# One-level Strassen in the up-projection of a transformer trunk, and the feed-forward in two phases

## The chip, the cores and the metric

The kernel runs on one NeuronCore of a Trainium2 chip, in one launch. The metric is the device time of one execution in microseconds. Engines are named as the profile names them: PE (TensorE, matmuls; PEld its weight loads), DVE (VectorE), ACT (ScalarE), POOL (GpSimd), SP (SyncE, which here only issues DMAs).

## What is computed

An inference step of a two-layer encoder for 1024 prompt rows and 8 x 16 sample rows (1152 rows of 1024 in all). Each layer has attention (layer 0: a sliding window with sinks; layer 1: a band over keys and values that all rows share) and a convolutional feed-forward. Every sub-layer gets a shift and a scale from a conditioning vector ("ada") and is closed by a LayerNorm. All is float32. The feed-forward, which the change is about (`w_up` goes from 1024 to 2 x 2816 channels, the convolution is causal over rows, by channel and three wide, `w_down` goes from 2816 back to 1024):

```python
def conv_ffn(h, prev, w_up, conv_w, conv_b, w_down):
    u = h @ w_up
    ...
    for tap in range(CONV_W):
        y = y + conv_w[tap] * ue[:, tap:tap + T]
    a, g = jnp.split(y, 2, axis=-1)
    out = (jax.nn.gelu(g) * a) @ w_down
    return out, ue[:, T:]
...
h = x * (1 + sc_f) + sh_f
f, conv_rows = conv_ffn(h, None if prompt else state_conv[l], w_up[l], conv_w[l], conv_b[l], w_down[l])
x = layer_norm(DEEPNORM_ALPHA * x + (1 + g_f) * f, ln_g[l, 1], ln_b[l, 1])
```

## The kernel before

Rows are 9 tiles of 128 (tiles 0 to 7 the prompt, tile 8 the samples). A product of float32 operands is three products of split operands: `split` makes a high part (a cast to fp32r, on ACT) and a low part (source minus high part, on DVE or POOL), and a product takes low x high, high x low and high x high.

The kernel is a straight program. A scheduler sets the order of the instructions on each engine ahead of the run, from its own estimates; each engine then runs its list strictly in order. All DMAs stand in SP's list. Stages: start and attention 0, output projection 0 (`out_proj`, which ends in a LayerNorm, `norm_tail`, and writes `H`, the split and transposed input of the feed-forward), feed-forward 0 (`ffn`), attention 1, output projection 1, feed-forward 1.

`H` is [part, channel block, 1152 rows]. `wload` brings 512 KB of weights into one of two staging slots (`ws`), casts them on ACT and subtracts on POOL (L151, L162) into one of four pairs of slots (`wh`, `wl`). In `ffn`, `up(j, gg)` multiplies one 128-channel tile of `w_up` (half gg of the GEGLU) with all rows in three blocks of 384 (`mmT`, L274, 24 matmuls a block), straight into convolution (`conv`: one activation on ACT, two taps on DVE that read PSUM), GELU and product (L1035, L1037); the result stays in SBUF. `down(g)` multiplies two finished tiles j with their rows of `w_down` (`dmm`, L1062, 6 matmuls of 512 columns for each tile of rows and half) and adds them to `acc` in SBUF (L1053 on DVE), for all nine tiles of rows; it runs among the next tiles' up-projection. `down_last` takes the last two j with the gate folded into the weights and finishes tile after tile with the LayerNorm. `pregate` adds the residual (L1121, L1122). `ada` makes the conditioning: seven of them, each 16 loads of 512 KB and 32 matmuls (L216). One stands at the start, two run beside attention 0, four (3 to 6) beside feed-forward 0 in steps (`step`, every `wload` takes 0.72 of a step).

Of the kernel before, what the change touches and what calls it, by code (L numbers as in the profile page):

```python
# [10 lines left out]
F32 = mybir.dt.float32  # L11
# [4 lines left out]
D = 1024  # L16
# [15 lines left out]
LO = ((0, 1, 2, 8, 3, 4, 5, 6, 7), (0, 1, 2, 3, 4, 5, 8, 6, 7))  # L32
UP = ({0: (0, 1), 2: (2,)}, {0: (0, 1), 3: (2,)})
LV = (0, 1, 2, 8, 3, 4, 5, 6, 7)
BGA = 0.33
BGF = 0.72
# [52 lines left out]
class Trunk:  # L89
    def __init__(self, ctx, tc, I, O):  # L90
# [10 lines left out]
        self.H = mem.tile([128, 2, 8, TOK], F32R, name="H")  # L101
# [21 lines left out]
        self.sm = ca.ring(16, 2)  # L123
        self.PS = psp.tile([128, 8, 512], F32, name="PS")
# [5 lines left out]
        self.oN = dr.tile([7, 128, 1024], F32, name="oN")  # L130
        self.oSD = dr.tile([8, 128, 128], F32, name="oSD")
# [136 lines left out]

    def mmT(self, w, out, s0, n):
        H = self.H  # L270
        i = 0
        for a, p in ((1, 0), (0, 1), (0, 0)):
            for k in range(8):
                self.nc.tensor.matmul(  # L274
                    out[:, 0:n], w[a][:, k * 128 : k * 128 + 128], H[:, p, k, s0 : s0 + n], start=i == 0, stop=i == 23
                )
                i += 1

    def mmX(self, out, t0, ws, kn, n):
# [3 lines left out]
        for j, w in enumerate(ws):  # L283
            for p, a in ((1, 0), (0, 1), (0, 0)):
                for k in range(kn):
                    self.nc.tensor.matmul(  # L286
                        out[:, 0:n],
                        H[:, p, j * kn + k, t0 : t0 + 128],
# [57 lines left out]
    def attention(self, l, wk):  # L346
# [5 lines left out]
        self.X1 = self.x1p.tile([128, 9216], F32R, name=f"x1att{l}", tag="x1")  # L352
        xa = Arena(self.X1)
# [50 lines left out]
        ka = Arena(self.F, (11136, 0)[l])  # L404
# [43 lines left out]
        def qblock(c, bi, w):  # L448
# [13 lines left out]
            for a in range(2):  # L462
# [23 lines left out]
        def scores(x):  # L486
# [9 lines left out]
            for qi in (2 * g, 2 * g + 1):  # L496
# [3 lines left out]
                q = qs(c, a, slice(0, 128), qi * 128, 128)  # L500
# [88 lines left out]
        def normalise(c, a, h):  # L589
# [146 lines left out]
        for i, x in enumerate(work):  # L736
# [12 lines left out]
            self.step(BGA)  # L749
# [601 lines left out]
```

## Time and profile before

| | us |
|---|---|
| median of 3 runs (2999.06 to 3001.47) | 3001.14 |
| span of the profiled execution | 3005.7 |
| PE busy | 2859.9 (95%) |
| DVE, ACT, POOL busy | 1563.2, 1162.4, 904.0 |
| mean granted clock of TensorE | 0.974 |

The profiled execution's span is 4.6 us longer than the median of the runs. In rows of groups the last three parts are busy us and mean ns of one, idle time before them, and what ended that. In rows of stages the numbers are busy us of PE, PEld, DVE, ACT and POOL with instruction counts, then the granted clock, the DMA engines' mean busy share and GB/s. A mean duration of a matmul is longer than what it costs, since matmuls are pipelined; costs are taken from stretches of many.

### The profile page before, as it was taken

What the parts mean: (1) busy time and instruction counts of PE and PEld (TensorE: products, weight loads), DVE (VectorE), ACT (ScalarE), POOL (GpSimd) and SP (SyncE); (2) the same over time, 40 slices, a digit from 0 to 9 for tenths busy, and PEclk for the clock granted to TensorE, in tenths of its full rate; (3) what the DMA queues carried; (4) which work ended last, traced back from release to release, by engine and by line L of the source; (5) the groups of instructions that cost most, each with busy time, mean ns of one, the idle gap of its engine ahead of it and who ended that gap; (6) DMA issues with size and microseconds to landing.
All of it is one profiled execution on the core that took longest, in us unless ns stands there. A gap on an engine that the chain in (4) does not pass through costs nothing.

```text
span 3005.7 us, 43456 instructions
## 1 busy us (share of the span) xinstructions
PE 2859.9 (95%) x16582; PEld 2548.1 (85%) x16582; DVE 1563.2 (52%) x3416; ACT 1162.4 (39%) x2608; POOL 904.0 (30%) x661
## 2 busy tenths in 40 slices
PE   7998889999999999998999999989999999999996
PEld 4986668888888898997999888867899999999985
DVE  4365658424444444458312677666624444444467
ACT  3464643332222222224435666652442222222224
POOL 2121322322222322253561111321422222222252
PEclk8998989999999999999999999999999999999998
DMA  8645353622222222222785467763311111111121
GB/s 299 186 145 155 107 158 111 224 88 78 99 88 81 101 76 74 79 84 101 266 296 180 116 158 196 189 203 108 131 43 41 43 44 45 43 43 43 42 78 66
DMA packets 175536, 353.96 MB, mean 118 GB/s; under 512 B 34632, under 2 KB 91784, under 8 KB 174944
## 3 DMA queue, kind: packets, MB, share of 16 engines
q1 hardware_dynamic: 175328, 351.19, 36.4%
q8 instruction: 130, 2.13, 0.3%
q14 instruction: 78, 0.64, 0.1%
HBM read 285.22 MB, written 75.35 MB: 120 GB/s over the span
## 4 chain that ended last, share of the span: by engine, by line
PE 70%; DVE 7%; ACT 3%; DMA 2%; issue 2%; POOL 2%; SPq 0%; DVEq 0%; ACTq 0%; POOLq 0%
PE PS L274 40%; PE PS L1062 16%; PE PS L286 7%; PE PS L559 1%; PE PS L540 1%; PE PS L216 1%; DVE acc L1122 1%; PE PS L514 1%; DVE F L480 1%; ACT F L784 1%; DMA oSD<-C 1%; DVE F L946 1%; PE PS L517 1%; PE PS L874 0%; POOL acc L1121 0%
## 5 line engine op out<-in xcount | busy, mean ns | idle before, releaser
L274 PE MATMUL PS<-H,wh 128*128 128x384 f32 x5472 | 1051.8, 337 | 0.3 <-DVE H L162 0.3
L274 PEld LDWEIGHTS PS<-H,wh 128*128 128x128 f32 x5472 | 964.2, 189 | 21.3 <-issue 5.4
L162 POOL TENSOR_TENSOR wl<-ws,wh 128x1024 fp32r<-128x1024 f32 x167 | 405.8, 2435 | 643.3 <-ACT wh L151 601.4
L274 PE MATMUL PS<-H,wl 128*128 128x384 f32 x2736 | 561.8, 342 | 38.0 <-POOL wl L162 9.8
L986 DVE SCALAR_TENSOR_TENSOR F<-PS,F 128x256 f32<-128x256 f32 (+2 forms) x704 | 352.7, 511 | 463.5 <-ACT F L983 453.1
L274 PEld LDWEIGHTS PS<-H,wl 128*128 128x128 f32 x2736 | 485.9, 190 | 71.7 <-issue 15.7
L1062 PE MATMUL PS<-wh,X 128*128 128x512 f32 x1320 | 420.1, 395 | 8.5 <-DVE acc L1053 3.2
L1053 DVE TENSOR_TENSOR acc<-acc,PS 128x512 f32<-128x512 f32 x324 | 221.6, 686 | 295.7 <-PE PS L1062 292.7
L1037 POOL TENSOR_TENSOR F<-F 128x384 f32<-128x384 f32 x132 | 136.4, 1033 | 729.5 <-ACT F L1035 719.9
L1062 PEld LDWEIGHTS PS<-wh,X 128*128 128x128 f32 x1320 | 245.1, 188 | 60.1 <-issue 9.2
L983 ACT ACTIVATE F<-PS,F 128x384 f32<-128x384 f32 x264 | 177.9, 674 | 243.7 <-PE PS L274 240.0
L151 ACT CAST wh<-ws 128x1024 fp32r<-128x1024 f32 x174 | 180.7, 1049 | 143.4 <-PE PS L1062 47.0
L1062 PE MATMUL PS<-wl,X 128*128 128x512 f32 x660 | 217.1, 394 | 0.0
L162 DVE TENSOR_TENSOR X<-F,X 128x384 fp32r<-128x384 f32 x110 | 125.4, 1140 | 117.1 <-ACT X L151 116.9
L1020 ACT COPY PS<-PS 128x2 f32<-128x2 f32 x176 | 25.6, 145 | 407.2 <-PE PS L274 388.2
L286 PE MATMUL PS<-wh,H 128*128 128x256 f32 (+1 forms) x936 | 173.1, 315 | 7.7 <-DVE H L162 7.2
L286 PEld LDWEIGHTS PS<-wh,H 128*128 128x128 f32 x936 | 137.3, 194 | 18.8 <-DVE H L162 7.8
L1062 PEld LDWEIGHTS PS<-wl,X 128*128 128x128 f32 x660 | 124.6, 189 | 28.5
L596 POOL TENSOR_TENSOR F<-F,x2att 64x512 f32<-64x512 f32 x62 | 79.3, 1279 | 202.7 <-DVE F L571 156.7
L540 PE MATMUL PS<-C,F 128*128 128x128 f32 x720 | 119.2, 287 | 18.4 <-DVE wh L546 8.0
L286 PE MATMUL PS<-x1att,H 128*128 128x512 f32 x504 | 133.2, 405 | 1.6 <-ACT x1att L151 1.4
L1035 ACT ACTIVATE F<-F 128x384 f32<-128x384 f32 x132 | 69.3, 525 | 145.7 <-DVE F L986 140.8
(212 smaller groups left out, 3574.8 us busy)
## 6 DMA issues: line engine op xcount, KB each, us to landing
ws<-in_wup_dram SPq DMA_DIRECT2D x88, 512.0 KB
F<-in_adaw_dram SPq DMA_DIRECT2D x74, 512.0 KB
ws<-in_wdn_dram SPq DMA_DIRECT2D x44, 512.0 KB
ws<-in_adaw_dram SPq DMA_DIRECT2D x32, 512.0 KB
x1att<-kH SPq DMA_DIRECT2D x60, 256.0 KB
xd<-F SPq DMA_DIRECT2D x27, 512.0 KB
F<-xd SPq DMA_DIRECT2D x27, 512.0 KB
vH<-X SPq DMA_DIRECT2D x40, 256.0 KB
```

What stands on the lines that cost most here:

```text
L151: nc.scalar.copy(out, in_)
L162: self.eng(el).tensor_sub(lo, src, hi.bitcast(F32))
L274: self.nc.tensor.matmul(out[:, 0:n], w[a][:, k * 128 : k * 128 + 128], H[:, p, k, s0 : s0 + n], start=i == 0, stop=i == 23)
L286: self.nc.tensor.matmul(out[:, 0:n], H[:, p, j * kn + k, t0 : t0 + 128], w[a][:, k * n : k * n + n], start=i == 0, stop=i == 23,)
L540: nc.tensor.transpose(t[:, m * 128 : m * 128 + 128], p[:, (kt - k0) * 128 : (kt - k0) * 128 + 128], self.ident)
L596: self.eng("v" if last else "p").tensor_mul(on[r, q], on[r, q], rb[r, :])
L983: nc.scalar.activation(y, ps[:, off : off + 384], AF.Identity, bias=w(3), scale=w(2))
L986: nc.vector.scalar_tensor_tensor(o, u, w(i), o, op0=ALU.mult, op1=ALU.add)
L1035: nc.scalar.activation(y, y, AF.Gelu_apprx_tanh)
L1037: nc.gpsimd.tensor_mul(a, y, ya[bi])
L1053: nc.vector.tensor_add(row[:, n], row[:, n], ps)
L1062: nc.tensor.matmul(ps, ac[m][p][:, cs], w[m][q][:, n], start=i == 0, stop=i == 5)
```

## The change

*Up-projection.* The channel tiles j and j + 22 (the two GEGLU halves) and the two halves of the 1024 input channels form a 2 x 2 block of weights; the rows form two sets q = 0, 1 (tiles 0 to 3 and 64 samples; tiles 4 to 7 and 64 samples), each of two halves of 288. For each j seven products of 512 channels x 288 rows take the place of eight. `forms` (for 128, 32 and 128 rows in turn) makes the seven right-hand combinations of the rows once a layer, behind (q = 1: in the midst of) the output projection, and splits each; they take the space of `H`, `X1` and `X2`. `prep(j)` makes and splits the seven left-hand combinations of the weights into nine slots (`fslots`). `unit(j, qs, w)` runs the products (`mm`, 12 matmuls each) into four PSUM banks a set, with copies and additions on ACT and DVE to `U` in SBUF. `tail(j)` does convolution, GELU and product from `U` and stores the tile to DRAM (`actD`). Units 0 and 1 run for q = 1 first, then for q = 0.

*Down-projection.* A phase of its own: for three groups of three row tiles, all 22 j in turn add up in six PSUM banks. Each (group, j) loads the weights (512 KB) and the activations (128 x 384) again and splits both. Three tiles are drained at a group's end (in the last group the last TAIL = 3 steps run tile by tile); the LayerNorm of groups 0 and 1 runs within the next group, that of group 2 at the end. The residual is stored before its LayerNorm affine, which `resid` now does on POOL.

*Else.* `H` is stored by tile ([part, tile, high or low, block, 128]). `ada` 3 moves to attention 0 (0.5 instead of 0.33 steps a pair there), 5 and 6 to attention 1, from the staging slots; only `ada` 4 stays, in the first down-phase. The bias table of layer 1 (`skew(1)`, 6 MB) moves from the start of feed-forward 0 to the start of its down-phase. `out_proj` takes the tiles in the order 4, 8, 6, 5, 7, 0, 2, 1, 3.

PE in the feed-forward, before (L274 up, L1062 down; `X_73`, `x2ffn` hold activations):

```order
L274 MATMUL PS<-H,wh 128x384
L1062 MATMUL PS<-wh,X_73 128x512
L1062 MATMUL PS<-wh,x2ffn_4493 128x512
L1062 MATMUL PS<-wl,X_73 128x512
L1062 MATMUL PS<-wl,x2ffn_4493 128x512
L1062 MATMUL PS<-wh,X_73 128x512
L1062 MATMUL PS<-wh,x2ffn_4493 128x512
L274 MATMUL PS<-H,wh 128x384 x3
```

and after, at the passage from the last unit (L1052) to the down-phase (L1178):

```order
L1052 MATMUL PS<-HX,wl 128x288 x4
L1052 MATMUL PS<-HX,wh 128x288 x8
L1052 MATMUL PS<-gup_3777,wl 128x288 x12
L1052 MATMUL PS<-HX,wl 128x288 x12
L1178 MATMUL PS<-wh,HX 128x512
L1178 MATMUL PS<-wl,HX 128x512
L1178 MATMUL PS<-wh,HX 128x512 x2
```

Up and down no longer alternate; within a unit the two sets do.

ACT in the feed-forward, before (L983 convolution out of PSUM, L1020 and L1031 short copies, L1035 GELU, L151 casts):

```order
L1020 COPY PS<-PS 128x2
L983 ACTIVATE F<-PS,F 128x384
L1020 COPY PS<-PS 128x2
L151 CAST wh<-ws 128x1024
L983 ACTIVATE F<-PS,F 128x384
L1031 COPY F<-PS 128x18
L983 ACTIVATE F<-PS,F 128x384
L1035 ACTIVATE F<-F 128x384
L151 CAST X_73<-F 128x384
L1020 COPY PS<-PS 128x2
L983 ACTIVATE F<-PS,F 128x384
L1035 ACTIVATE F<-F 128x384
```

and one unit after (L1070, L1076, L1081 out of PSUM for the seven products; L1027 casts of the next unit's weights; L1097, L1098, L1119 the tail of the unit before):

```order
L1070 COPY F<-PS 128x288
L1119 ACTIVATE F<-F 128x1152
L1070 COPY F<-PS 128x288
L1027 CAST wh<-F 128x512 x2
L1076 COPY F<-PS 128x288 x2
L1027 CAST HX<-ws 128x512
L1027 CAST wl<-F 128x512
L1081 COPY F<-PS 128x288 x2
L1027 CAST wh<-F 128x512
L1027 CAST wh<-ws 128x512
L1097 ACTIVATE F<-F 128x1024
L1098 ACTIVATE F<-F 128x128
```

The tail of one unit stands among the copies and casts of the next.

POOL in the feed-forward, before (L162 weights, L1001 and L1037 the GEGLU, L237 ada):

```order
L162 TENSOR_TENSOR wl<-ws,wh 128x1024
L1001 TENSOR_TENSOR F<-F 128x8x2
L1037 TENSOR_TENSOR F<-F 128x384 x2
L162 TENSOR_TENSOR wl<-ws,wh 128x1024 x2
L237 TENSOR_SCALAR F<-F 32x512 x2
```

and after, from the last tail of layer 0 (L1120) into the down-phase (L175 weights, L1196 and L1197 the residual's affine, `x1dn` the residual):

```order
L1111 TENSOR_TENSOR F<-F 128x8x2
L175 TENSOR_TENSOR wl<-ws,wh 128x1024
L1120 TENSOR_TENSOR F<-F 128x1152
L175 TENSOR_TENSOR wl<-ws,wh 128x1024
L1196 TENSOR_TENSOR x1dn_9682<-x1dn_9682,F 128x1024 x3
L1197 TENSOR_TENSOR x1dn_9682<-x1dn_9682,F 128x1024
L175 TENSOR_TENSOR wl<-ws,wh 128x1024
L1197 TENSOR_TENSOR x1dn_9682<-x1dn_9682,F 128x1024 x2
L175 TENSOR_TENSOR wl<-ws,wh 128x1024 x16
```

The six affine operations of the first group stand behind the fifth load.

The diff, cut to its core:

```diff
-BGA = 0.33
-BGF = 0.72
+BGA = (0.5, 0.33)
+BGF = 0.5
+ORD = (4, 8, 6, 5, 7, 0, 2, 1, 3)
+GRP = ((0, 1, 2), (3, 4, 5), (6, 7, 8))
+P1, P2, P6, P5, P7, P4, P3 = range(7)
+NB = 288
...
     def out_proj(self, l, xsrc, xdst, aff):
...
-        for t in (8, 0, 1, 2, 3, 4, 5, 6, 7):
+        for i, t in enumerate(ORD):
...
+            if i == 4:
+                self.forms(1, hb, (4, 6), (5, 7))
+        self.forms(0, hb, (0, 2), (1, 3))
+    def forms(self, q, hb, *pairs):
...
+        for ha, oa, hx, ob, c0, n in jobs:
...
+            def put(f, src, el):
+                hi, lo = (self.form(q, f, p)[:, :, c0 : c0 + n] for p in range(2))
+                nc.scalar.copy(hi, src)
+                self.eng(el).tensor_sub(lo, src, hi.bitcast(F32))
+
+            put(P1, b11, "p")
+            put(P2, b21, "p")
+            nc.vector.tensor_sub(t1, b12, b11)
+            nc.vector.tensor_sub(t2, b22, t1)
+            put(P6, t2, "v")
+            put(P5, t1, "p")
+            nc.vector.tensor_sub(t3, b22, b12)
+            nc.vector.tensor_sub(t4, b21, t2)
+            put(P7, t3, "v")
+            put(P4, t4, "p")
+            put(P3, b22, "p")
...
+    def up_phase(self, l):
+        def prep(j):
...
+            w[P1] = put(a11, "p")
+            w[P2] = put(a12, "p")
+            nc.vector.tensor_add(s1, a21, a22)
+            nc.vector.tensor_sub(s2, s1, a11)
+            w[P6] = put(s2, "v")
+            w[P5] = put(s1, "p")
+            nc.vector.tensor_sub(s4, a12, s2)
+            nc.vector.tensor_sub(s3, a11, a21)
+            w[P7] = put(s3, "p")
+            w[P4] = put(a22, "p")
+            w[P3] = put(s4, "v")
...
+        def unit(j, qs, w):
+            for f in range(7):
+                for q in qs:
+                    if f == P1:
+                        mm(Z, w, q, f, True)
+                        nc.scalar.copy(ca, Z)
+                    elif f == P2:
+                        mm(X, w, q, f, True)
+                        nc.vector.tensor_add(u0[2 * q], X, ca)
+                    elif f == P6:
+                        mm(Z, w, q, f, False)
+                        nc.scalar.copy(cb, Z)
...
+        def tail(j):
+            for gg in range(2):
+                nc.gpsimd.tensor_copy(u[:, 1:4, 0:2], u[:, 0:3, 256:258])
+                nc.scalar.activation(yp, u[:, :, 2:258], AF.Identity, bias=w(3), scale=w(2))
+                nc.scalar.activation(ys, u[:, :, 258:290], AF.Identity, bias=w(3), scale=w(2))
+                tap(yp, u[:, :, 1:257], 1)
+                tap(yp, u[:, :, 0:256], 0)
...
+            nc.scalar.activation(Y[1], Y[1], AF.Gelu_apprx_tanh)
+            nc.gpsimd.tensor_mul(Y[1], Y[1], Y[0])
+            nc.sync.dma_start(self.actD[j], Y[1])
+        w0 = prep(0)
+        unit(0, (1,), w0)
+        w1 = prep(1)
+        unit(1, (1,), w1)
...
+        unit(1, (0,), w1)
+        tail(1)
+        w0 = prep(0)
+        unit(0, (0,), w0)
+        tail(0)
+        for j in range(2, NFF):
+            unit(j, (1, 0), prep(j))
+            tail(j)
+    def down_phase(self, l, xsrc, xdst, affs):
...
+        def load(g, j):
+            w = self.wload(I["wdn"][l, j])
+            nc.sync.dma_start(r, self.actD[j][:, g * 384 : g * 384 + 384])
+            self.split(r, *h, "a", "v")
...
+        for g, ts in enumerate(GRP):
+            final = g == len(GRP) - 1
+            nt = TAIL if final else 1
+            for j in range(NFF - nt):
+                w, h = load(g, j)
+                for i, t in enumerate(ts):
+                    mm(w, h, t, i, j)
+                if g == 0 and j == 2:
+                    self.ln_consts(l, 1)
+                    self.ln_rows(l, 0, ga, ba)
...
+                        self.skew(1)
+                if todo and j % 4 == 3:
+                    finish(*todo.pop(0))
+            xs = [resid(t) for t in ts]
...
+            for i, t in enumerate(ts):
...
```

More of the change, by code (lines that the diff above doesn't have):

```diff
@@ L274, in mmT @@
                 self.nc.tensor.matmul(
[L275 removed]
+                    out, w[a][:, k * 128 : k * 128 + 128], self.Hx(p, k, s0, n), start=i == 0, stop=i == 23
                 )
@@ L367, in attention @@
         pts = Ring(pts)
-        x2b = self.x2p.tile([128, 768], F32, name=f"x2att{l}", tag="x2b")
-        rb, olo = x2b[:, 0:512], x2b[:, 512:768]
+        ga = Arena(self.G)
+        rb, olo = ga.take(512), ga.take(256)
         fa = Arena(self.F)
         sKt = fa.take(2176)
-        sV = fa.take(1536)
+        sV = ga.take(1536)
         on = fa.take(1024)
@@ L894, in norm_tail @@
-        if er is None:
-            nc.sync.dma_start(xdst[sl, :], x)
-            return
-        xr = xrr.next() if xrr else x
-        self.eng(er[0]).tensor_mul(xr, x, self.lng)
-        self.eng(er[1]).tensor_add(xr, xr, self.lnb)
-        nc.sync.dma_start(xdst[sl, :], xr)
+        G, B = aff
+        for hf in range(2):
+            ps = self.bank(tb.next())
+            for c in range(4):
+                nc.tensor.transpose(
+                    ps[:, c * 128 : c * 128 + 128], x[:, (hf * 4 + c) * 128 : (hf * 4 + c) * 128 + 128], self.ident
+                )
+            if t < 8:
+                for c in range(4):
+                    cc = hf * 4 + c
+                    src = ps[:, c * 128 : c * 128 + 128]
+                    if save and cc in VA:
+                        nc.vector.tensor_scalar(
+                            h3[:, cc, :], src, G[:, cc, 0:1], B[:, cc, 0:1], op0=ALU.mult, op1=ALU.add
+                        )
+                    else:
+                        nc.scalar.activation(h3[:, cc, :], src, AF.Identity, bias=B[:, cc, 0:1], scale=G[:, cc, 0:1])
+            else:
+                self.sample_affine(h3[:, hf * 4 : hf * 4 + 4, :], self.tiles(ps), G, B, hf * 4, 4, "v")
+            if save:
+                nc.scalar.copy(self.zt[:, hf * 512 : hf * 512 + 512], ps)
@@ L1042, in down @@
-        def down(g):
-            js = (2 * g, 2 * g + 1)
-            w = [self.wload(I["wdn"][l, j]) for j in js]
-            for t in range(NT):
-                row = acc[:, t * 1024 : t * 1024 + 1024]
-                for hf in range(2):
-                    n = slice(hf * 512, hf * 512 + 512)
-                    ps = dmm(js, w, t, n)
-                    if g == 0:
-                        nc.scalar.copy(row[:, n], ps)
-                    else:
-                        nc.vector.tensor_add(row[:, n], row[:, n], ps)
@@ L1115, in ffn @@
-        prering = Ring([self.hf, self.xr])
-        def pregate():
-            for t in range(NT):
-                x = self.residual(t, xsrc, prering)
-                row = acc[:, t * 1024 : t * 1024 + 1024]
-                nc.gpsimd.tensor_mul(row, row, self.gateP if t < 8 else self.gateS)
-                nc.vector.scalar_tensor_tensor(row, x, ALPHA, row, op0=ALU.mult, op1=ALU.add)
-        NG = NFF // 2
-        for g in range(NG):
-            up(2 * g, 0)
-            if g == 1:
-                self.ln_consts(l, 1)
-            if g > 0:
-                down(g - 1)
-            if g == NG - 1:
-                self.drain()
-                pregate()
-            up(2 * g, 1)
-            if g < NG - 1:
-                up(2 * g + 1, 0)
-                up(2 * g + 1, 1)
```

478 lines of the change are left out of this document (253 added, 225 removed).

## The prediction

> **What bounds the kernel now.** I read the page first (busy shares, granted clock, the chain that ended last), then the stages, then the chain of work in order of time for prices, then groups and single instructions for the engines that must keep up.
>
> The page:
>
> ```profile
> span 3005.7 us, 43456 instructions
> PE 2859.9 (95%) x16582; PEld 2548.1 (85%) x16582; DVE 1563.2 (52%) x3416; ACT 1162.4 (39%) x2608; POOL 904.0 (30%) x661
> PEclk8998989999999999999999999999999999999998
> PE 70%; DVE 7%; ACT 3%; DMA 2%; issue 2%; POOL 2%; SPq 0%; DVEq 0%; ACTq 0%; POOLq 0%
> ```
>
> TensorE is busy 95% of the span and carries 70% of the chain: what leaves TensorE leaves the time, where nothing else then comes late. The busy times by stage (columns: PE, PEld, DVE, ACT, POOL, granted clock, DMA share, GB/s) say where:
>
> ```profile
> 150.00:417.00 267.00, 240.49 (x1721) 188.07 (x1720) 167.95 (x588) 153.97 (x461) 84.25 (x76) 0.92 0.46 137
> 527.00:1316.00 789.00, 783.15 (x4213) 705.24 (x4212) 333.02 (x553) 230.26 (x459) 227.85 (x177) 1.00 0.28 97
> 1316.00:1446.00 130.00, 112.39 (x586) 99.60 (x585) 106.34 (x205) 52.80 (x107) 65.66 (x35) 0.95 0.34 121
> 1446.00:2004.00 558.00, 534.88 (x3905) 491.18 (x3904) 292.17 (x898) 320.02 (x754) 169.04 (x119) 0.99 0.68 202
> 2131.00:2881.00 750.00, 743.09 (x3938) 699.60 (x3937) 329.38 (x543) 231.31 (x460) 218.46 (x165) 1.00 0.15 49
> 2881.00:3005.70 124.70, 93.28 (x434) 81.10 (x432) 97.63 (x175) 41.55 (x74) 53.57 (x28) 0.90 0.21 78
> ```
>
> Both feed-forwards (rows two and five) are TensorE alone, at full clock. Their ends (rows three and six) are not: DVE is as busy as TensorE while nine tiles are finished one after another.
>
> Prices and stage borders, from single instructions and from the chain in order of time (start, us, what):
>
> ```profile
> 526.71 1.55 PE L274 MATMUL PS<-H,wl 128*128 128x384 f32 x8
> 2130.33 1.38 PE L274 MATMUL PS<-H,wl 128*128 128x384 f32 x7
> 1199.44 0.99 PE PS L216 x8
> 1394.90 0.87 PE PS L874 x8
> 1446.15 6.22 PE PS L286 x48
> 1453.24 2.87 PE PS L286 x24
> 1565.55 56.40 PE PS L286 x468
> 2159.76 46.04 PE PS L274 x264
> 2205.80 4.12 PE PS L1062 x18
> ```
>
> A matmul of 384 columns costs 46.04/264 = 0.1744 us, one of 512 4.12/18 = 0.2289, one of 256 2.87/24 = 0.1196 (0.1205 in the long stretch), a 128-column transpose 0.109. Layer 0's feed-forward runs from 526.7 to 1446.2, 919.4 us; its matmul work is 3168 x 0.1744 + 1188 x 0.2289 + 4 ada x 3.96 + 96 transposes x 0.109 = 851. So 68 us are lost. Layer 1: 2130.3 to 3005.7, 875.4 us, work 827 (no ada, 24 transposes), 48 lost.
>
> **The change, part by part.**
>
> *Up-projection.* Per pair of channel tiles, 2 x 3 x 24 = 144 matmuls of 384 become 7 x 2 x 12 = 168 of 288. No row has 288; between 256 and 384 lies 0.1196 + (0.1744 - 0.1196)/4 = 0.1333. I take it, since 256 is near. Ends: in proportion to columns, 0.1308; no cheaper than 384, 0.1744. The weight load is no floor here: it goes at 0.109 behind the transposes. A unit is 168 x 0.1333 = 22.4 us against 144 x 0.1744 = 25.1: 44 units save 119 us (ends: 138 saved, 185 lost).
>
> *What must hide beside a unit.* Groups (mean ns of one before the second bar) and one undisturbed 1024-wide operation:
>
> ```profile
> L162 POOL TENSOR_TENSOR wl<-ws,wh 128x1024 fp32r<-128x1024 f32 x167 | 405.8, 2435 | 643.3 <-ACT wh L151 601.4
> L1037 POOL TENSOR_TENSOR F<-F 128x384 f32<-128x384 f32 x132 | 136.4, 1033 | 729.5 <-ACT F L1035 719.9
> L596 POOL TENSOR_TENSOR F<-F,x2att 64x512 f32<-64x512 f32 x62 | 79.3, 1279 | 202.7 <-DVE F L571 156.7
> L151 ACT CAST wh<-ws 128x1024 fp32r<-128x1024 f32 x174 | 180.7, 1049 | 143.4 <-PE PS L1062 47.0
> L1053 DVE TENSOR_TENSOR acc<-acc,PS 128x512 f32<-128x512 f32 x324 | 221.6, 686 | 295.7 <-PE PS L1062 292.7
> 1322.45 1.23 DVE L1122 SCALAR_TENSOR_TENSOR acc<-F,acc 128x1024 f32<-128x1024 f32 x1 [1.55 <-POOL acc L1121]
> ```
>
> Estimates per unit. ACT: 7 casts of 512 at 0.6, 6 copies of 288 and the tail's three activations, 11 us. POOL: 5 subtractions at 1.28, one 1152-wide product 2.7, eight small ones 1.6, 10.7. DVE: 8 additions out of PSUM at 0.5 = 4.0; four 1024-wide taps at 1.2, eight short ones at 0.2, six 512-wide at 0.69, together 10.5. Each fits in 22.4. The order places a unit's taps, then POOL's product, then the next weights, and a form's weights are due five forms (16 us) after their slot comes free, so I charge 0.4 us a unit, 9 a layer. Ends 0 and 2.5 a unit: 2.5 if DVE and POOL take turns, which these rows (DVE twice, then POOL) suggest:
>
> ```profile
> 2325.35 2.19 DVE L162 TENSOR_TENSOR X<-F,X 128x384 fp32r<-128x384 f32 x1 [0.78 <-ACT X L151]
> 2339.33 0.56 DVE L162 TENSOR_TENSOR X<-F,X 128x384 fp32r<-128x384 f32 x1 [2.28 <-ACT X L151]
> 2324.73 2.39 POOL L162 TENSOR_TENSOR wl<-ws,wh 128x1024 fp32r<-128x1024 f32 x1
> ```
>
> The same subtraction takes 0.56 us alone, and 2.19 when it starts inside a POOL subtraction, ending just behind it. The taps now read both operands from SBUF, where before one was in PSUM, so they join this queue. [...]
>
> *Start of the up-phase.* Before, these waits (in brackets) and the slow matmuls behind the longer one:
>
> ```profile
> 537.81 1.62 PE L274 MATMUL PS<-H,wl 128*128 128x384 f32 x8 [1.71 <-ACT PS L1020]
> 546.97 2.93 PE L274 MATMUL PS<-H,wl 128*128 128x384 f32 x8 [3.88 <-ACT H L151]
> 546.97 7.12 PE PS L274 x24
> ```
>
> 24 matmuls took 7.12 us behind a wait of 3.88, 2.9 over price: about 9 us lost in all. Now `forms(0)` (10 subtractions at 1.28 and five short ones on POOL), two `prep` (10 x 1.28) and the sample-state products (4 us) stand before the first unit that reads q=0: some 31 us of POOL and 20 of DVE (24 subtractions at 0.69 and two tiles' norms), partly taking turns, against three half units (34 us) and 8 us of earlier cover. I charge 15 a layer (ends 6 and 35). [...]
>
> *Down-projection.* The same 1188 matmuls, so 272 us. DVE's 324 additions (221.6 us) go, off the path. In exchange each of 66 (group, j) steps a layer loads 512 KB of weights and 192 KB of activations and splits both for 18 x 0.2289 = 4.12 us of matmuls. Two staging slots: load, cast 1.05, POOL 2.4. The load, then a saturated stretch of DMA, and what an ada step costs from the staging slots and the wait for the sample heads:
>
> ```profile
> 1319.72 3.29 DMA ws<-in_wdn_dram
> 560.00:565.00 5.00, 5.00 (x30) 5.00 (x29) 1.47 (x3) 2.58 (x5) 1.46 (x2) 1.00 1.00 378
> L216 PE MATMUL PS<-ws,C 128*32 128x512 f32 x128 | 23.9, 704 | 8.1 <-DMA ws<-in_adaw_dram 8.1
> PE PS L286 <- DVE H L162: 5.2, 1, 5.2
> ```
>
> 3.29 + 1.05 + 2.4 + hops of 0.2 = 6.95 a slot, 3.5 a step from two: under 4.12, with little to spare. The affine of the residual (18 POOL operations of 2.4 a layer) and layer 0's splits delay it: 10 us in layer 0, 8 in layer 1 (ends 0 and 25). Group 0 is worse. On POOL the residual's affine stands behind the fifth load and waits for LayerNorm rows whose buffer the last tail still reads; SP's queue waits with it. In layer 0 the ada weights (8.4 MB), the 6.3 MB bias table, gates, rows and residuals (4.7 MB) come on top of 16 MB: 35 MB need over 93 us even at 378 GB/s, and the group has 91 us of matmuls. I charge 22 and 10 (ends 10 to 45, 4 to 25).
>
> *Ends.* Six tiles are finished under the next group's matmuls, three behind the last: gate, sum, statistics, store, some 14 us a layer (ends 10 and 25); most of what rows three and six lose goes.
>
> *Attention and output projection.* Three of four ada leave feed-forward 0, 12 us of matmul; from the staging slots each costs (23.9 + 8.1)/4 = 8 us, in stages where TensorE has 27 and 23 us idle, so I charge 18 of 24. The sample tile goes second instead of first: the 5.2 us wait goes, -6. Net +12 (ends -6 and +30). The tiled layout of H splits the 384 moving columns of 1872 matmuls into three runs: nothing taken, since bytes and columns stay (ends 0 and three 128-column matmuls each, +286).
>
> *Sum.* Layer 0: 22 x 22.4 + 272 + 4 + 10 + losses (15 + 9 + 22 + 10 + 14) = 849, 70 less than 919. Layer 1: 493 + 272 + 3 + losses (15 + 9 + 10 + 8 + 14) = 824, 52 less than 875. With +12: 110 less, a span of 2895. The profiled span is 4.6 us above the runs' median of 3001.1, so the median becomes 2891 us.
>
> **The rivals.**
>
> 1. DVE and POOL pace the units. Their exclusive work is 10.5 + 10.7, and DVE's PSUM additions add 4.0: up to 25.2 us a unit against the 22.8 charged, 44 x 2.4 = 106 more: 2997 at worst, and 2976 when a fifth of the excess overlaps, which I give. For: the rows above. Against: the order lets POOL idle during the taps.
> 2. Slower: the loads pace the down-phase. The place is the two staging slots. It decides from a step of 4.12 + (110 + 18)/132 = 5.1 us on, a landing of 6.5 us instead of 3.29. At 8 us a step takes 5.8 and the time is 2891 + 132 x 1.7 - 18 = 3097. For: two loads, activations and POOL in one loop. Against: 0.7 MB per 4.12 us is 171 GB/s, under half of the saturated row.
> 3. The losses stay at their lower ends (28 and 20 instead of 70 and 56): 2813. For: each has idle engines around it.
> 4. The change doesn't do what it says: 288 columns, or three runs, cost more than columns say. A unit at 0.1744 takes 29.3 and the time is 3195. Against: 256 costs 0.1196.
>
> **How the numbers follow.** Forecast (own range 2830 to 2955) 0.65, rival 1 0.13, rival 2 0.07, rival 3 0.10, rival 4 0.02; 0.03 lies between rivals 1 and 2 near the old time. Predicted 2891 us; the range 2815 to 2985 leaves out part of rival 3 and the rest above. Within 0.2% is 6 us, about what a measurement of this kernel can tell from no change: faster 0.88, same 0.03, slower 0.09.
>
> **What would show it.** 288-column matmuls at 0.133 in the chain; units of 22.4 to 23 us with TensorE above 97% and full clock; 18-matmul steps every 4.1 to 4.3 us in groups 1 and 2; a hole of some 20 us in layer 0's group 0 with DMA share near 1; about 14 us behind the last matmul. Wrong it would be by units near 25 with TensorE waiting for DVE's or POOL's weights, by down steps above 5 us ended by POOL's `wl`, or by a 288-column price above 0.15.

## The result, and the profile after

The changed kernel takes 3136.7 us (median of 4 runs, 3132.9 to 3139.8) against 3001.3 beside it: 1.0445 times as long, 95% interval 1.0427 to 1.0462. The forecast was 2891 us. It was wrong in sign, and the time lies above its range.

The page of the profiled execution, the counterpart of the lines shown of before:

```profile
span 3135.2 us, 47797 instructions
PE 2800.1 (89%) x17638; PEld 2459.1 (78%) x17638; DVE 1885.9 (60%) x3559; ACT 1345.4 (43%) x2780; POOL 1451.0 (46%) x1135
PEclk8999889999999989989999999989999999999898
```

TensorE has 60 us less to do than before (2859.9), as meant, and is idle for 335 us instead of 146. DVE rose from 1563 to 1886, POOL from 904 to 1451.

Where the time went is read between borders at which both kernels start the same work: the first matmul of each feed-forward, and one matmul of attention 1. The two feed-forwards of before start at 526.71 and 2130.33 us, as the prediction shows; the matmul of attention 1 in before, then the three of after (start, us, what):

```profile
1562.41 0.63 PE L286 MATMUL PS<-wh,H 128*128 128x256 f32 x4
```

```profile
549.64 0.70 PE L1052 MATMUL PS<-HX,wh 128*128 128x288 f32 x4
1611.33 0.64 PE L305 MATMUL PS<-wh,HX 128*128 128x256 f32 x4
2231.87 0.70 PE L1052 MATMUL PS<-HX,wh 128*128 128x288 f32 x4
```

| from border to border, us | before | after | difference | forecast |
|---|---|---|---|---|
| start to feed-forward 0 | 526.7 | 549.6 | +22.9 | +12 with the third row |
| feed-forward 0, to attention 1 under way | 1035.7 | 1061.7 | +26.0 | -70 |
| rest of attention 1, output projection 1 | 567.9 | 620.5 | +52.6 | (in the first row) |
| feed-forward 1 to the end | 875.4 | 903.3 | +27.9 | -52 |

So the forecast misses 64 us in the attentions and 96 and 80 in the feed-forwards, 240 in all. The stages of after (busy us of PE, PEld, DVE, ACT, POOL, then clock, DMA share, GB/s): up- and down-phase 0, attention 1, up- and down-phase 1, and 100 us of steady units:

```profile
549.60:1093.30 543.70, 503.45 (x3714) 496.75 (x3714) 384.26 (x596) 241.25 (x436) 325.78 (x327) 0.99 0.21 76
1093.30:1458.40 365.10, 308.78 (x1305) 239.24 (x1305) 186.37 (x180) 121.59 (x181) 247.23 (x107) 0.92 0.64 220
1614.20:2231.80 617.60, 558.14 (x3874) 472.01 (x3873) 357.11 (x1028) 321.05 (x766) 127.00 (x111) 0.96 0.59 173
2231.80:2776.10 544.30, 505.03 (x3714) 498.37 (x3713) 385.83 (x596) 241.05 (x436) 324.92 (x327) 0.99 0.21 76
2776.10:3117.70 341.60, 294.62 (x1190) 235.34 (x1188) 203.75 (x162) 112.51 (x157) 218.07 (x92) 0.92 0.48 162
2400.00:2500.00 100.00, 93.16 (x694) 91.97 (x693) 69.19 (x112) 44.53 (x79) 56.22 (x60) 1.00 0.18 67
```

An up-phase takes 544 us where 517 were charged, layer 1's down-phase 341.6 where 293 were, the tail behind it 17.5 (14 charged).

What TensorE waited for, in up-phase 1, in the down-phase behind it, and in attention 1 (us in total, times, longest):

```profile
PE PS L1052 <- ACT F L1070: 24.2, 17, 2.0
```

```profile
PE PS L1178 <- ACT wh L164: 18.5, 5, 7.2
PE PS L1178 <- DVE HX L175: 13.7, 5, 6.6
PE PS L1178 <- POOL wl L175: 9.3, 3, 7.3
```

```profile
PE PS L229 <- DMA ws<-in_adaw_dram: 16.8, 8, 6.2
PE PS L256 <- DVE ws L243: 5.5, 2, 5.1
```

*The down-phase.* The starts of its matmuls give the length of each of layer 1's 66 steps (the last three of group 2 are one tile after another), in us:

```
group 0  4.1 4.1 4.1 4.1 5.5 14.3 4.3 4.1 4.1 4.1 4.1 4.1 4.1 4.1 4.1 4.1 4.1 4.1 4.1 4.1 4.1 6.3
group 1  6.3 5.2 4.1 10.9 6.7 7.3 7.7 7.0 8.2 4.1 4.1 4.1 4.1 4.1 4.1 4.1 4.1 4.1 4.1 4.1 4.1 6.9
group 2  5.8 4.1 4.1 8.1 7.3 11.5 6.4 8.9 7.4 4.1 4.1 4.1 4.1 4.1 4.1 4.1 4.1 4.1 4.1 6.3 4.1 3.9
```

44 of the 66 take 4.1 us, which their matmuls need (18 x 0.2289 = 4.12). In these the loads keep up. The loss is 13, 29 and 28 us a group. It stands at the groups' ends and in the steps in which the residual's affine and, in groups 1 and 2, three tiles' LayerNorm run. In the first 45.2 us of group 1 (2879.8 to 2925.0, some six and a half steps) the main groups of DVE and POOL read, with shapes kept apart (busy us, mean ns of one, idle before):

```profile
L175 DVE TENSOR_TENSOR HX<-F,HX 128x384 fp32r<-128x384 f32 x7 | 12.2, 1755 | 7.0 <-ACT HX L164 7.0
L1203 DVE CUSTOM_DVE_ANT_0 x1dn<-x1dn 128x1024 f32<-128x1024 f32 x3 | 7.4, 2476 | 0.0
L831 DVE TENSOR_TENSOR C<-C 128x1 f32<-128x1 f32 x3 | 3.6, 1209 | 0.0
L856 DVE SCALAR_TENSOR_TENSOR x1dn<-x1dn,C,F 128x1024 f32<-128x1024 f32 x1 | 3.3, 3329 | 0.0
L1192 DVE TENSOR_TENSOR x1dn<-PS,x1dn 128x512 f32<-128x512 f32 x5 | 3.2, 676 | 0.0
L827 DVE RECIPROCAL C<-C 128x1 f32<-128x1 f32 x3 | 0.4, 147 | 0.0
```

```profile
L175 POOL TENSOR_TENSOR wl<-ws,wh 128x1024 fp32r<-128x1024 f32 x6 | 15.3, 2542 | 3.9 <-ACT wh L164 3.9
L1197 POOL TENSOR_TENSOR x1dn<-x1dn,F 128x1024 f32<-128x1024 f32 x3 | 8.3, 2787 | 0.0
L1196 POOL TENSOR_TENSOR x1dn<-x1dn,F 128x1024 f32<-128x1024 f32 x3 | 7.9, 2621 | 5.0 <-DMA x1dn<-xd 5.0
```

This is the clearest picture of the cause. A product of two numbers a partition (L831) takes 1.2 us in the mean, and a reciprocal of one number 0.15. The long ones here have two operands in SBUF and run while POOL is busy: L175's subtraction, 0.55 us with POOL idle, takes up to 2.76. L1192, which reads one of its two from PSUM, takes 0.68 (0.67 to 0.69 over all 36 of the trace), also beside POOL. Two of the sums of row and residual (L1203, both operands in SBUF), one with POOL idle and one that starts just behind a POOL instruction, show it singly:

```profile
2889.56 1.21 DVE L1203 CUSTOM_DVE_ANT_0 x1dn<-x1dn 128x1024 f32<-128x1024 f32 x1
2891.09 2.41 POOL L1196 TENSOR_TENSOR x1dn<-x1dn,F 128x1024 f32<-128x1024 f32 x1 [4.40 <-DMA x1dn<-xd]
2891.17 3.41 DVE L1203 CUSTOM_DVE_ANT_0 x1dn<-x1dn 128x1024 f32<-128x1024 f32 x1
```

The second ends 1.08 us behind POOL's instruction, about its own length of 1.21. At what each form takes undisturbed elsewhere in the trace, DVE's two-operand work in this stretch is 11.9 us (7 x 0.55, six of 1.2 to 1.3, five of 0.15) and POOL's 33: together 45 us, the whole stretch, in which TensorE got through 120 matmuls, 27.5 us.

One wait, of 6.63 us, cost more than itself; the matmuls behind it, and the stage of these 5.3 us:

```profile
2906.23 2.93 PE L1178 MATMUL PS<-wh,HX 128*128 128x512 f32 x6 [6.63 <-DVE HX L175]
```

```profile
2906.20:2911.50 5.30, 5.27 (x12) 4.14 (x13) 5.15 (x9) 0.72 (x1) 4.53 (x2) 0.50 0.14 37
```

The clock granted was 0.50: 12 matmuls took 5.3 us instead of 2.75, 2.5 us lost.

### The profile page after: what moved, and what is told of

The parts are those of the page before. It is cut to its first block, busy times and chain, and to the rows that moved or that the text cites. A ratio compares the mean times of both kernels' runs of the same rounds, so it can differ in the third digit from the quotient of the medians.

```text
span 3135.2 us, 47797 instructions
## 1 busy us (share of the span) xinstructions
PE 2800.1 (89%) x17638; PEld 2459.1 (78%) x17638; DVE 1885.9 (60%) x3559; ACT 1345.4 (43%) x2780; POOL 1451.0 (46%) x1135
## 5 line engine op out<-in xcount | busy, mean ns | idle before, releaser
L175 POOL TENSOR_TENSOR wl<-ws,wh 128x1024 fp32r<-128x1024 f32 x171 | 418.7, 2452 | 478.3 <-ACT wh L164 441.1
L1178 PE MATMUL PS<-wh,HX 128*128 128x512 f32 x1584 | 523.4, 410 | 61.1 <-ACT wh L164 36.6
L175 DVE TENSOR_TENSOR HX<-F,HX 128x384 fp32r<-128x384 f32 (+2 forms) x163 | 288.6, 1780 | 311.9 <-ACT HX L164 300.6
L1178 PEld LDWEIGHTS PS<-wh,HX 128*128 128x128 f32 x1584 | 312.9, 199 | 139.6 <-ACT wh L164 40.9
L1052 PE MATMUL PS<-HX,wh 128*128 128x288 f32 x2656 | 405.8, 297 | 7.4 <-ACT F L1070 5.6
L1052 PEld LDWEIGHTS PS<-HX,wh 128*128 128x128 f32 x2656 | 371.9, 190 | 9.0 <-ACT F L1070 6.6
L1101 DVE SCALAR_TENSOR_TENSOR F<-F 128x1024 f32<-128x1024 f32 x528 | 337.7, 699 | 37.0 <-POOL F L1113 34.6
L1178 PE MATMUL PS<-wl,HX 128*128 128x512 f32 x792 | 325.1, 411 | 24.5 <-POOL wl L175 24.5
L1052 PE MATMUL PS<-HX,wl 128*128 128x288 f32 x1592 | 266.2, 299 | 55.5 <-ACT F L1070 31.5
L1052 PEld LDWEIGHTS PS<-HX,wl 128*128 128x128 f32 x1592 | 229.1, 190 | 64.5 <-ACT F L1070 37.2
L293 PE MATMUL PS<-HX,wh 128*128 128x384 f32 x1248 | 246.2, 340 | 0.1
L293 PEld LDWEIGHTS PS<-HX,wh 128*128 128x128 f32 x1248 | 219.9, 191 | 3.8 <-issue 1.7
L1178 PEld LDWEIGHTS PS<-wl,HX 128*128 128x128 f32 x792 | 157.0, 198 | 68.8 <-POOL wl L175 33.1
L1097 ACT ACTIVATE F<-F 128x1024 f32<-128x1024 f32 x88 | 109.5, 1244 | 214.8 <-DVE F L1085 109.2
L1028 POOL TENSOR_TENSOR wl<-ws,wh 128x512 fp32r<-128x512 f32 x94 | 133.9, 1425 | 117.5 <-ACT wh L1027 117.5
L1052 PE MATMUL PS<-x1att,wh 128*128 128x288 f32 x1160 | 177.7, 297 | 0.0
L1052 PEld LDWEIGHTS PS<-x1att,wh 128*128 128x128 f32 x1160 | 162.6, 189 | 0.0
L305 PEld LDWEIGHTS PS<-wh,HX 128*128 128x128 f32 x936 | 137.7, 196 | 27.8 <-POOL HX L175 5.7
```

Of the source, the lines that this page charges most:

```text
L175: self.eng(el).tensor_sub(lo, src, hi.bitcast(F32))
L293: self.nc.tensor.matmul(out, w[a][:, k * 128 : k * 128 + 128], self.Hx(p, k, s0, n), start=i == 0, stop=i == 23)
L305: self.nc.tensor.matmul(out[:, 0:n], H[:, t0 // 128, p, j * kn + k, :], w[a][:, k * n : k * n + n], start=i == 0, stop=i == 23,)
L1028: self.eng(el).tensor_sub(lo, src, hi.bitcast(F32))
L1052: nc.tensor.matmul(out, w[f][a][:, k * 128 : k * 128 + 128], x[:, k, :], start=start and i == 0, stop=i == 11, skip_group_check=True,)
L1097: nc.scalar.activation(yp, u[:, :, 2:258], AF.Identity, bias=w(3), scale=w(2))
```

## The experiments

Each is an edit of the changed kernel. "Faster by" is the difference of its ratio to 1.0445, times 3001 us; a ratio's interval is 0.0013 to 0.004 (4 to 12 us) to either side.

**Finish later (d_spread).**

```diff
-                if todo and j % 4 == 3:
+                if todo and j % 6 == 5:
```

> Only the times at which finished tiles get their LayerNorm in the down-phase change: at steps 5, 11 and 17 of the next group instead of 3, 7 and 11. In the changed kernel the steps of groups 1 and 2 take 4.1 us except in the first eleven, and the four groups with a finish lose 28.6, 28.0 (layer 1), 19.9 and 31.7 us (layer 0). Theory P (DVE and POOL take turns, and residual affine, weight split, activation split and LayerNorm together need more than the matmul time while a finish runs): POOL's residual affine stays at the group's start, the rest gets spread, so the four losses fall from 108 to 50 to 70 us in all and the time falls by 40 to 60 us. Rival L (the residuals' loads stand ahead of the weights in SP's queue and the two staging slots run dry): those loads stay where they are, 0 to 10 us.

3139.3 us, ratio 1.0461 (1.0421 to 1.0502): no change. The long steps of layer 1's group 1 lay at steps 3 to 8 as before: the scheduler left the finishing work where it was. The edit did not do what it should, so this run decides nothing.

**Weight split on DVE (d_dve).**

```diff
-            w = self.wload(I["wdn"][l, j])
+            w = self.wload(I["wdn"][l, j], el="v")
```

> The low part of the down-phase's weights is made on DVE (128x1024, about 1.23 us alone) instead of POOL (2.4 us). Theory P: time in which one of the two shuts the other out falls from 2.95 to 1.8 us a step; the finishing groups' losses (108 us in all) fall by a third to a half, 40 to 55 us faster. Rival L (loads): a slot comes free 1.2 us sooner, but the late loads behind the residuals stay, 0 to 15 us faster. Third: DVE's queue is strictly in order, and the weights' split now stands behind LayerNorm work there, so that matmuls wait longer: 0 to 40 us slower.

3040.1 us, ratio 1.012 (1.0094 to 1.0147): 97 us faster, more than any theory gave. Layer 1's groups lose 4.5, 7 and 8.5 us in place of 13, 29 and 28. The loads stand where they stood, so rival L is out; DVE, which now carries more, is not late, so the third is out as well. POOL's list gets shorter here as well as the time in which the two exclude each other; d_resid, below, parts these.

**The order of the products (u_order).**

```diff
-            for f in range(7):
+            for f in (P1, P2, P5, P6, P7, P4, P3):
```

> In a unit of the up-phase the product P5 (another PSUM bank) is run ahead of P6, so that the product which adds to P1's bank starts 3.2 us later. Theory U (TensorE waits 1.4 us a unit for ACT's copy of P1, which stands on ACT behind the former unit's convolution, itself behind DVE's late last addition): the waits for L1070 (48 us in all) go, steady units fall from 23.9 to 22.6-22.8 us, 40 to 50 us faster. Rival T (DVE and POOL pace the units): the wait turns up elsewhere, in P7 or at the weights, 0 to 10 us faster.

3141.6 us, ratio 1.0467 (1.0434 to 1.05). The waits for L1070 went, and 50.2 us of waits for L1081, the copy of P7, came in their place; steady units still took 23.9 to 25. That fits T, but P6 and P7 now also stand side by side on one bank, with less time for the copy between them, so this run alone doesn't settle it.

**ada 5 and 6 in the down-phase (a_down), with four score banks kept (a_banks).**

```diff
-            self.bg = [self.ada(4, 7, fr)]
+            self.bg = [self.ada(i, 7, fr) for i in (4, 5, 6)]
...
-        self.bg = [self.ada(5, 4), self.ada(6, 4)]
+        self.bg = []
```

and in a_banks besides

```diff
-            if not self.bg and len(sbk.items) == 4:
+            if l == 0 and not self.bg and len(sbk.items) == 4:
```

> ada 5 and 6 move from attention 1 into layer 0's down-phase, behind ada 4 and with its buffers. From the first score matmul to the end of output projection 1 the changed kernel is 53 us longer than before. Theory A (the two ada cost that: 25 us of matmuls in the path, 22 us of waits for their loads and rows): attention 1 falls by 45 to 53 us, the down-phase pays 25 us of matmuls and perhaps some delayed loads, net 15 to 28 us faster. Rival H (the tiled layout of H, or the larger DMA volume, makes attention longer): attention 1 stays within 10 us of 53 over, net 15 to 25 us slower.

> As the run with ada 5 and 6 in the down-phase, but attention 1 keeps four score banks instead of five. Theory A1 (the 53 us were the ada's matmuls and the waits for their loads): as that run, 37 us faster than the changed kernel (30 to 40). Theory A2 (the missing fifth bank held the scores up): attention 1 keeps 20 us or more of the 53, so 0 to 17 us faster.

3099.4 and 3097.7 us, both ratio 1.0317: 38 us faster. From the last matmul of down-phase 0 to feed-forward 1 it takes 718 us instead of 774; down-phase 0 pays 15.6 us. So an ada costs 28 us beside attention 1 by these two traces and 8 us in the down-phase. (In the runs that leave attention 1 as it is, this stretch takes 763 to 770 us, by which it is 23 to 26.) The fifth score bank is worth nothing here, and the three-run layout of `H` isn't the cause. The latter stands in the matmuls too (ns min/median/max), of before and after in attention 1:

```profile
L274 PE MATMUL PS<-H,wh x768: 331/334/443, 1457.3 to 1924.9; 128*128 128x384 f32 x192
```

```profile
L293 PE MATMUL PS<-HX,wh x768: 331/334/442, 1479.1 to 2020.7; 128*128 128x384 f32 x192
```

**All low parts of the up weights on DVE (u_dve)**, five such lines:

```diff
-            w[P1] = put(a11, "p")
+            w[P1] = put(a11, "v")
```

> In the up-phase the low parts of all seven weight combinations are made on DVE (0.68 us each) instead of five on POOL (1.3 us). Reordering the products left the steady unit at 23.9 us and only moved the wait to another copy. Theory T (DVE and POOL shut each other out and pace the unit): 6.5 us a unit less of exclusive POOL time for 3.4 more on DVE, units fall to 22.6 to 23.2 us, and the start (two units with forms beside them) shortens by 5 to 10 us a layer: 35 to 70 us faster. Theory U (only the place of ACT's copy behind the former unit's convolution and DVE's taps counts): DVE's queue gets 3.4 us longer, the copy no earlier, units 23.9 to 25: 0 to 45 us slower.

3100.4 us, ratio 1.033 (1.0308 to 1.0351): 35 us faster, the up-phases 528 us instead of 544, steady units about 23.5. U expected a loss; T is right in sign, with the time at its lower end and units above the 22.6 to 23.2 that it gave.

**The tail written later (u_late).**

```diff
+                if f == P6 and mid is not None:
+                    tail(mid)
...
-            unit(j, (1, 0), prep(j))
-            tail(j)
+            unit(j, (1, 0), prep(j), j - 1 if j > 2 else None)
+        tail(NFF - 1)
```

> The former unit's tail (convolution, taps, GELU, product) is written behind the first two products of the next unit, so that ACT's copies of P1 and DVE's last additions come ahead of it; the work is the same. Theory U: the waits for L1070 (48 us in all) go and turn up nowhere else, steady units of 22.4 to 22.8 us: 40 to 55 us faster. Theory T: units stay at 23.9 us, the wait shows at another copy, addition or weight: within 10 us.

Ratio 1.0452 (1.043 to 1.0473), no change, and none in the order: ACT's list had the convolution ahead of P1's copy as before. It tells nothing.

**Without the wide taps (u_notap).**

```diff
-                tap(yp, u[:, :, 1:257], 1)
-                tap(yp, u[:, :, 0:256], 0)
```

> Leaves out the four 1024-wide taps a unit (two of the convolution's three taps over the prompt rows), 4 x 1.35 us of DVE with both operands in SBUF. Both theories T and U expect units of 22.4 to 22.8 us, 45 to 60 us faster in all; a rival by which the matmuls themselves cost more among other work (reads of the same memory, gaps between accumulation groups) expects units of 23.5 to 23.9 us and under 15 us.

3056.3 us, ratio 1.0174 (1.0152 to 1.0195): 81 us faster where 45 to 60 were expected, 70 of it in the two up-phases. Units take 22.3 us (168 x 0.1327), TensorE without a gap:

```profile
2400.00:2500.00 100.00, 100.00 (x755) 100.00 (x754) 43.98 (x100) 46.58 (x80) 45.55 (x63) 1.00 0.22 77
```

The matmuls cost what was forecast. The gaps come from the work beside them.

**Taps forced behind the last addition (u_force).**

```diff
-                        nc.vector.tensor_add(u0[2 * q + 1], Yb, cb)
+                        self.lastadd = nc.vector.tensor_add(u0[2 * q + 1], Yb, cb).ins
...
                 def tap(o, v, i):
+                  with self.tc.issue_after(self.lastadd):
```

> u_late left the order on ACT and DVE as it was (the scheduler sorts by its own estimates), so it told nothing. Here the order is forced: all taps of a unit stand on DVE behind the unit's last addition out of PSUM, the same work otherwise; ACT's convolution of the second half then starts earlier, and the copies of P1 follow it sooner. Theory U (the late last addition makes ACT's copies late): the steady unit falls from 23.9 to 22.3-22.7 us as without taps, 40 to 70 us faster. Theory T (DVE and POOL are the pace, 69 and 56 us of 100 busy, in turns): 23.5 to 24 us a unit, within 15 us.

3126.0 us, ratio 1.0406 (1.038 to 1.0432). The order is as meant now, and the up-phases take 542.9 us each (543.6 and 544.2 without): U is out. The 12 us gained lie between the two up-phases; their cause stays open. The order only chooses which instruction meets the delay.

**The residual's affine on DVE (d_resid).**

```diff
-            nc.gpsimd.tensor_mul(x, x, ga)
-            nc.gpsimd.tensor_add(x, x, ba)
+            nc.vector.tensor_mul(x, x, ga)
+            nc.vector.tensor_add(x, x, ba)
```

> The residual's affine in the down-phase (6 products or sums of 128x1024 a group) moves from POOL (2.4 us each) to DVE (1.23); the weights' split stays on POOL. Theory P (DVE and POOL exclude each other): 7.2 us less exclusive time a group, the six groups lose 5 to 9 us less each, 30 to 50 us faster. Rival Q (POOL's own queue is full while a finish runs, 14.4 us of affine and eleven weight splits of 2.4 in 45 us of matmuls, and sharing has no part): the 14.4 us leave POOL, the finishing groups lose almost nothing more, 75 to 100 us faster. Spread of the LayerNorm work in time had no effect to judge by, since the order moved by a step or two only.

3094.0 us, ratio 1.0308 (1.0284 to 1.0333): 41 us faster. P gave 30 to 50, Q 75 to 100: POOL's own length isn't the whole of it. Groups 1 and 2 of layer 1 still lose 18 and 20 us (29 and 28 without the edit), where Q had them lose almost nothing.

**Together: split, ada, bias table (b_down); then the up-phase too (best1); then POOL's last wide work (best2); then ada 3 (best3).** b_down is d_dve, a_down, and `tables_b` at the start with `skew(1)` written by rows:

```diff
             unit(j, (1, 0), prep(j))
+            if l == 0 and j < 18:
+                self.skew(1, j - 2)
```

best1 adds u_dve and u_force; best2 adds d_resid and

```diff
-            nc.gpsimd.tensor_mul(Y[1], Y[1], Y[0])
+            nc.vector.tensor_mul(Y[1], Y[1], Y[0])
```

and best3 `self.ada(i, 7, fr) for i in (3, 4, 5, 6)`, with `BGA = (0.33, 0.33)`, `BGF = 0.65` and `affine(*affs)` at `g == 1, j == 0`.

> Three edits together: the down-phase's weight split on DVE (alone 97 us faster), ada 5 and 6 in layer 0's down-phase (alone 37 us faster), and layer 1's bias table (6 MB) written in sixteen pieces in layer 0's up-phase, whose DMA share is 0.21, instead of in the third step of the down-phase, where 18.2 us of waiting for weights are left with the split on DVE. If the three have separate causes the sum holds: 97 + 37 + 15 = 149 us faster than the changed kernel, about 2988 us. If ada and bias table both stand for the same crowding of DMA in layer 0's down-phase, the ada's 25 MB take back 10 to 20 us there: about 3005 us.

> All together: split of the down weights on DVE, ada 5 and 6 in the down-phase, the bias table in the up-phase (2990 us so far), all low parts of the up weights on DVE (36 us alone) and the taps behind the last addition. Theory U: up-phases fall from 545 to 505-515 us each, 2915 to 2930 us. Theory T: to 525-530 each, 2950 to 2960 us.

> On top of the last version, POOL's remaining wide work beside matmuls moves to DVE: the product of a unit's tail (1152 wide, 2.67 us on POOL, about 1.4 on DVE) and the residual's affine in the down-phase. What is read is each stage for itself. Theory P/T (exclusion by POOL's wide operations): units go from 23.2 to 22.3-22.7 us (another 10 to 18 us in all), the twelve-us steps in groups 1 and 2 shrink to 6 or less (15 to 25 us in all), 2900 to 2917 us. Rival O (in-order queues alone: what counts is how much stands on DVE, whoever runs beside it): DVE carries 1.4 us a unit and 7 us a group more, units 23.2 to 23.8, steps no shorter, 2935 to 2955 us.

> In addition ada 3 goes from attention 0 into layer 0's down-phase, ahead of 4, 5 and 6, at 0.65 steps a pair, and attention 0 goes back to 0.33; the LayerNorm affine that needs it is made at group 1's start. Theory A (an ada beside attention costs some 25 us, 12.4 of them matmuls): start to output projection 0 gets 20 to 25 us shorter, the down-phase 12 to 20 longer, 3 to 12 us faster than the version ahead of it. Rival (the +23 us of attention 0 are another part of the change, such as the three-run layout): attention 0 stays, 10 to 20 us slower.

| | median us | ratio to before (95%) |
|---|---|---|
| b_down | 2990.4 | 0.996 (0.9947 to 0.9974) |
| best1 | 2940.9 | 0.979 (0.977 to 0.9811) |
| best2 | 2876.9 | 0.9581 (0.9558 to 0.9605) |
| best3 | 2862.6 | 0.9535 (0.9508 to 0.9561) |

b_down's sum held (2988 expected). The hole that the bias table makes was, in the changed kernel, this wait, with this DMA in these 37 us and the DMA engines 97% busy:

```profile
1150.47 2.93 PE L1178 MATMUL PS<-wh,HX 128*128 128x512 f32 x6 [14.13 <-ACT wh L164]
```

```profile
q1 hardware_dynamic: 4135, 12.38, 96.8%
...
skb<-eb SPq DMA_DIRECT2D x1, 6144.0 KB
```

In b_down no wait over 1.3 us is left in that group. d_dve, which leaves the bias table where it is, keeps a wait of 18.2 us there, so it was not the split that took the hole away; the ada's edit brings more loads into that group, which leaves the table's as the likely one of b_down's three edits.

best1 tells little of U against T (units 23.2, the time between the two ranges); best2 decides. Steady stretches of best1 and best2, and best2's up-phase 1 and down-phase 1:

```profile
2400.00:2500.00 100.00, 96.64 (x720) 95.45 (x718) 81.02 (x135) 43.73 (x79) 27.18 (x42) 1.00 0.19 67
```

```profile
2400.00:2500.00 100.00, 100.00 (x754) 100.00 (x754) 79.32 (x144) 48.22 (x82) 16.68 (x39) 1.00 0.22 74
2084.20:2586.50 502.30, 495.73 (x3714) 494.56 (x3713) 414.53 (x732) 248.60 (x436) 102.88 (x191) 1.00 0.24 82
2586.50:2858.80 272.30, 269.61 (x1189) 222.63 (x1188) 175.10 (x244) 112.34 (x157) 14.92 (x8) 1.00 0.60 204
```

From the fourth on all units are 22.3 us, and groups 1 and 2 of layer 1 have 4.1 us in each step, with more on DVE than ever (415 us in the up-phase against 386): rival O is out. Theory P/T is right in sign and too small: against best1 the up-phases are 35 us shorter and the down-phases 38, where 10 to 18 and 15 to 25 were expected. The same operations of DVE in the finishing steps of best2 (2679.6 to 2724.8):

```profile
L175 DVE TENSOR_TENSOR HX<-F,HX 128x384 fp32r<-128x384 f32 x10 | 5.5, 547 | 0.0
L1206 DVE CUSTOM_DVE_ANT_0 x1dn<-x1dn 128x1024 f32<-128x1024 f32 x3 | 3.6, 1215 | 0.0
L1200 DVE TENSOR_TENSOR x1dn<-x1dn,F 128x1024 f32<-128x1024 f32 x3 | 3.6, 1213 | 0.0
```

547 ns in place of 1755, 1215 in place of 2476. best3 starts feed-forward 0 at 533.2 us instead of 560.3 and pays 8.3 us in down-phase 0, so the 22.9 us in the first row of the table from border to border were ada 3: attention 0 paid about as much for its ada as attention 1. best3 is the fastest version, 4.65% under the kernel before.

## Why the prediction was wrong, point by point

Of the 240 us by which the span missed the forecast's sum, 145 stand in the up-phases (54) and in groups 1 and 2 of the down-phases (91), where the prediction took DVE's and POOL's work as hidden for the most part, and 64 in the attentions, where it had the price of an ada too low.

- *Price of a 288-column matmul, 0.1333, unit 22.4 us.* Right: 24.20 us for 180 in the row below, 0.1344 with small gaps, and 22.3 us a unit where nothing disturbs. Rival 4 is out.

```profile
2737.73 24.20 PE PS L1052 x180
```

- *"I charge 0.4 us a unit".* This step failed first. A steady unit lost 1.6 us. The prediction had the sum for it (rival 1: DVE and POOL, 25.2 us a unit in turns) and the rows of the exclusion, and set them aside with "the order lets POOL idle during the taps". That the taps join this queue stands in after: one of 1024 at 625.9 us, started inside a POOL subtraction (L1028, 625.77 to 627.09), took 2.32 us, those beside it 1.27; in before, with one operand in PSUM, none of the 704 taps (L986) took over 0.62. u_force shows that forcing the order of the taps doesn't matter; best2 that POOL's wide work does. The two up-phases together became 82 us shorter on the way from after to best2 (544.2 + 543.6 to 502.3 + 503.3). In the up-phase the runs don't part exclusion from POOL's slower instructions and the buffers they hold (in after DVE also sat idle for POOL's `wl` before L1040, 92.1 us in 28 waits); both left together, so that part stays open.
- *Start of the up-phase, 15 a layer.* 24 to 25 in after (53 us over 22 x 22.3, less the steady loss), 12 in best2: the charge was some 10 us a layer too low, and half of what was lost went with POOL's wide work.
- *Groups 1 and 2, "10 us in layer 0, 8 in layer 1".* The largest miss: 52 and 57 us. The prediction looked for the danger in the loads (a staging slot every 3.5 us), which d_dve leaves where they are while layer 1's 57 us fall to 15, and counted the finish as hidden "under the next group's matmuls". It didn't add up DVE's and POOL's work there, 45 us in turns where 27.5 us of matmuls ran, though it had placed every piece of it. Rival 1 was asked for the units only; it was decided in the down-phase as well.
- *Waits at their length.* The prediction counted slow matmuls behind a wait at the start of the up-phase (2.9 us), but none in the down-phase. Layer 1's down-phase is 69 us shorter in best2 (341.6 to 272.3). Of that, idle time is 44 us and TensorE's busy time 25 (294.62 to 269.61), the clock at 0.92 against 1.00. Charged at their idle time alone, these stalls would come out 25 us too low.
- *Group 0, 22 and 10 us.* Within its ends: 33 (132.1 less 90.6 of matmuls and 8 of ada) and 13; the hole stood where the prediction put it, with the bias table as its likely cause.
- *Ends, 14.* 17.5 behind the last matmul. In layer 0 some 12 us are left for its end beyond the charge when the other terms are taken off its 96; no run looks into them.
- *Attention, +12.* Wrong by 64, and the term was mis-sized. The row `x128 | 23.9, 704 | 8.1` was divided by four, as 32 records an ada. It has 64 (448 for seven), so the same row gives 16 us each, 48 for three, and in place they cost 23 to 28 each, 76 in all:

```profile
L229 PE MATMUL PS<-ws,C 128*32 128x512 f32 x128 | 24.7, 660 | 16.8 <-DMA ws<-in_adaw_dram 16.8
```

  24.7 us of matmuls and 22 of waits for two. That attention had idle time of its own (27 and 23 us) didn't help: an ada's matmuls came in the path, and its loads had to wait for staging slots which the ada's own matmuls still read (16.5 us in seven waits of SP's queue in attention 1).
- *Work of 851 us in layer 0, four ada at 3.96.* The same halving: 8 of 64 records took 0.99 us, so an ada's matmuls take 7.9, the work was 867 and 52 us were lost, not 68. a_down's 15.6 us for two and best3's 8.3 for one bear it out; in the changed kernel ada 4 took 8 us where 4 were charged.
- *Three-run layout, nothing.* Right: 334 ns before and after.
- *Rival 2, loads.* Out: 44 of 66 steps at 4.1 us. *Rival 3* out.

With POOL's wide work gone, the price of the work itself holds: feed-forward 1 of best2 takes 502.3 + 272.3 + 16.9 = 791.5 us. The forecast charged 824, 768 of work and 56 of losses, of which 24 are left.

## What to carry to other kernels

Before moving work beside matmuls, add up for each stretch between two waits what DVE does with two SBUF operands and what POOL does, as one engine (11.9 + 33 us in the 45.2 us above), and compare with the matmul time of that stretch and not with the phase. Where the sum comes near, the step to try first is to move POOL's wide elementwise work to DVE, at half the time (1.23 us against 2.4 for 128x1024); here that turned a loss of 4.45% into a gain of 4.65%, with three ada put back beside the down-projection, where each costs 8 us, and one 6 MB transfer cut into pieces. And count a group's records per job before dividing a row by jobs.

## What the runs showed of the hardware that was not expected

- A DVE product of two 128x1 operands in SBUF (L831) took 1.2 us in the mean in a stretch in which POOL was busy (1.94 at most), and 0.15 at the least. The most that such an operation took there above its shortest was 2.2 us at each of three sizes: 128x1 (L858, 2.30 against 0.15), 128x384 (L175, 2.76 against 0.55), 128x1024 (L1203, 3.41 against 1.21).
- After a wait of 6.6 us TensorE ran 5.3 us at clock 0.50, 2.5 us lost.
- DVE was busy for 414.5 of 502.3 us in best2's up-phase 1 with little wide work left on POOL, and from the fourth unit on TensorE had no gap.
